# An MLP run per half of the tokens, with its up-projection as seven block products instead of eight

## The chip, the cores and the metric

One core of one Trainium2 chip runs the whole program. The metric is the device time of one execution in microseconds; the kernel before has a median of 2911.13 us over 3 runs (2910.79 to 2911.31).

## What is computed

Two layers of a small hybrid network over 1152 tokens (128 context tokens, then 1024 latent tokens) of width 1024. Each layer is a token mixer (attention, linear attention and a recurrent branch) and then an MLP with a hidden width of 4096 and squared ReLU:

```python
    h = rmsnorm(x, P['norm2'][l]) * (1.0 + sc2) + sh2
    u = jax.nn.relu(h @ P['w_mlp1'][l])          # 1024 -> 4096
    x = x + g2 * ((u * u) @ P['w_mlp2'][l])      # 4096 -> 1024
```

Scale, shift and gate differ between context and latent tokens. Only this part changes; the mixer, the final norm and the other outputs stay.

## The kernel before

Activations lie with the channels on the partitions: `x[k]` (k = 0 to 7) is 128 channels x 1152 tokens in SBUF. All large products are done in float32r (`F32R`) with a two-term split: each fp32 operand is cast to a high part (`wh`, `hh`, `uh`) and the rest is its low part (`wl`, `hl`, `ul`). One product of two 128-wide blocks is then three matmuls, high by high, high by low and low by high: lines 156, 157 and 158 of `dense`. `load_w` brings 1024 columns of weights by one DMA on SP's queue (`wr`), ACT casts them (L119), DVE takes the rest (L120).

The tokens are worked in three thirds of 384 (`TB`); `parts` cuts the first third at token 128, where scale and shift change. In `mlp`:

- `norm2(tb)` makes the modulated activations of one third, channel block by channel block (`norm`, L350 to L358), as a generator whose steps are put in between matmuls by `tick`. It needs the reciprocal root mean square of that third: `squares` (L300 to L306), the transposes L313 in `rstd`, the power L318 on POOL, and `spread` (L331 to L338), which spreads it over the partitions.
- `up_prep(f)` loads one 128-column tile f of the up-weights (32 tiles), `up_unit(f, tb)` multiplies it with one third (8 channel blocks x 3 matmuls of 384 columns) and makes ReLU and squares: ACT L1259 and L1260, POOL L1261, DVE L1262.
- `down_chunk(c, tbs)` multiplies four finished tiles with the down-weights (L1283 adds the gated result to x on DVE). Up and down are interleaved, four tiles at a time. `last_tb` starts the next layer's first norm for a third when its last chunk is done.

A weight tile is loaded and split once per layer and used for all three thirds. The first up tiles of a layer run third by third, so that the norm of the second and third thirds is made while the matmuls of the first run. `post_out` drives the end of the mixer's output projection (`out_half`, L1218 to L1225) and adds the norms as their thirds become ready.

PE's order is the order in which the code emits the matmuls. The order on DVE, ACT and POOL is made by a scheduler from the dependences and is fixed at build time; each of these engines runs its list in that order.

Of the kernel before, what the change touches and what calls it, by code (L numbers as in the profile page):

```python
# [7 lines left out]
F32 = mybir.dt.float32  # L8
F32R = mybir.dt.float32r
AF = mybir.ActivationFunctionType  # L10
ALU = mybir.AluOpType
# [3 lines left out]
D = 1024  # L15
KD = 8
TP = 128
# [2 lines left out]
NT = T // 128  # L20
TB = 384
NTB = T // TB
DEPTH = 2
DFF = 4096
EPS = 1e-6
# [22 lines left out]


class Net:  # L50
# [1177 lines left out]
    def mlp(self, l, post_out, last_tb, side_work=None):  # L1228
        nc, I = self.nc, self.I
        hg, hp = self.open(f"h2_{l}", bufs=1)  # L1230
        hh = [hp.tile([128, T], F32R, tag=f"hh{k}", name=f"hh{k}") for k in range(KD)]
        hl = [hp.tile([128, T], F32R, tag=f"hl{k}", name=f"hl{k}") for k in range(KD)]
        M = self.M[l]
        N2 = {}

        def norm2(tb):
            N2[tb] = self.add(self.norm(self.xa, tb, self.rs2, lambda: M["G2"], lambda: M["sh2"], lambda kt, b: blk(hh[kt], b),
                                        lambda kt, b: blk(hl[kt], b)))

        post_out(norm2)  # L1240
        ug, up = self.open(f"u_{l}", side="right", bufs=5)
        NF = DFF // 128
        CH = 4
        U = {}
        self.wide = True
        W = {}

        def up_prep(f):
            W[f] = self.load_w(I["w_mlp1"][l, :, f * 128:f * 128 + 128].rearrange("(k p) c -> p k c", p=128), KD)
            U[f] = (up.tile([128, T], F32R, tag="uh", name="uh"), up.tile([128, T], F32R, tag="ul", name="ul"))  # L1250

        def up_unit(f, tb):
            wh, wl = W[f]
            uh, ul = U[f]
            p = self.pd()
            self.dense(p[:, :TB], [wh[:, k] for k in range(KD)], [wl[:, k] for k in range(KD)],
                       [(blk(hh[k], tb), blk(hl[k], tb)) for k in range(KD)], True)
            r = self.te()
            nc.scalar.activation(r, p[:, :TB], AF.Relu)  # L1259
            nc.scalar.activation(blk(uh, tb), r, AF.Square)  # L1260
            nc.gpsimd.tensor_tensor(r, r, r, ALU.mult)  # L1261
            nc.vector.tensor_tensor(blk(ul, tb), r, f32(blk(uh, tb)), ALU.subtract)  # L1262

        def up_tile(f):
            up_prep(f)
            for tb in range(NTB):
                up_unit(f, tb)

        def down_chunk(c, tbs):
            fs = range(c * CH, c * CH + CH)  # L1270
            for dp in range(KD // 2):
                wh, wl = self.load_w(I["w_mlp2"][l, c * CH * 128:(c + 1) * CH * 128, dp * 256:dp * 256 + 256]
                                     .rearrange("(k p) c -> p k c", p=128), CH)
                for dd in range(2):
                    dt = 2 * dp + dd
                    for tb in tbs:
                        p = self.pd()
                        sl = slice(128 * dd, 128 * dd + 128)
                        self.dense(p[:, :TB], [wh[:, k, sl] for k in range(CH)], [wl[:, k, sl] for k in range(CH)],
                                   [(blk(U[f][0], tb), blk(U[f][1], tb)) for f in fs], True)  # L1280
                        for a, b, s in parts(tb):
                            xa = self.xa(dt, tb)[:, a:b]
                            nc.vector.scalar_tensor_tensor(xa, p[:, a:b], self.M[l]["g2"][:, dt, s:s + 1], xa, ALU.mult, ALU.add)  # L1283

        for f in range(2):
            up_prep(f)
        for tb in range(NTB):
            self.finish(N2[tb])
            for f in range(2):
                up_unit(f, tb)  # L1290
        if side_work:
            self.add(side_work())
        for f in range(2, CH + 1):
            up_tile(f)
        nch = NF // CH
        for c in range(nch):
            if c == nch - 1:
                self.drain()
                self.close(hg)
                for tb in range(NTB):  # L1300
                    down_chunk(c, [tb])
                    last_tb(tb)
            else:
                down_chunk(c, range(NTB))
            for f in range((c + 1) * CH + 1, min((c + 2) * CH + 1, NF)):
                up_tile(f)
        self.close(ug)

    def final_open(self):
# [74 lines left out]
    def layer(self, l, depth):  # L1384
        self.mixer(l)
        side = self.mod_round(l, 2, self.pe, slow=3)
        seq = [(0, 1), (1, 1), (2, 1), (0, 0), (1, 0), (2, 0)]
        done, state = set(), {"gen": None, "left": 0, "cur": None}
        nc = self.nc
        self.rs2 = {}  # L1390
        rs0 = self.norm_rs(self.xa, 0, self.rs2)

        def load_next(force):
            if seq and seq[0] not in self.ms and (force or seq[0][1] or seq[0][0] in done):
                assert seq[0][1] or seq[0][0] in done
# [36 lines left out]
        def post_out(norm2):  # L1432
            done.add(2)
            load_next(False)
            for _ in rs0:
                pass
            added = 0
            k = 0
            while out_step():
                k += 1  # L1440
                if added == 0:
                    norm2(0)
                    added = 1
                if added == 1 and (1, 0) not in seq and state["cur"] == (2, 0):
                    self.chain.insert(0, self.norm_rs(self.xa, 1, self.rs2, eng0=nc.vector))
                    norm2(1)
                    added = 2
                if k % 2 == 0:
                    self.tick()
            self.chain.insert(0, self.norm_rs(self.xa, 2, self.rs2, eng0=nc.vector))  # L1450
            norm2(2)
# [89 lines left out]
```

## Time and profile before

| | |
|---|---|
| median of 3 runs | 2911.13 us |
| profiled execution, its own time | 2908.05 us |
| its span in the profile | 2906.2 us |
| mean granted TensorE clock | 0.977 |
| PE busy | 2748.9 us (95%), 16067 matmuls |
| DVE, ACT, POOL busy | 1455.2 us (50%), 1119.6 us (39%), 802.5 us (28%) |

In a row, `x2006` is a count of instructions; shapes are partitions x elements. Matmuls are pipelined: a row's duration of one matmul is longer than the distance to the next one, so what a stream of matmuls costs is read from starts, or from a count in a stretch without idle time.

### The profile page before, as it was taken

The numbers are of one execution on the slowest core, as the hardware profiler recorded it, in microseconds if no ns is written. First come the engines' busy times: TensorE is split into PE (matmuls) and PEld (weight loads), VectorE is DVE, ScalarE is ACT, GpSimd is POOL, SyncE is SP. The second block draws the span as 40 slices with busy tenths as digits, with TensorE's granted clock in tenths as the row PEclk, the third lists the DMA queues.
The fourth block names the chain that finished last, engine by engine and source line by source line (L and its number), as shares of the span: only waits on it lengthen the run. The fifth ranks groups of instructions, "written<-read, shape, count | busy, mean of one in ns | idle before, by whom it ended". The sixth has DMA issues, their size and how long they took to land. (4 is left out here: it accounts for less than half of the span.)

```text
span 2906.2 us, 41527 instructions
## 1 busy us (share of the span) xinstructions
PE 2748.9 (95%) x16067; PEld 2625.6 (90%) x16067; DVE 1455.2 (50%) x2577; ACT 1119.6 (39%) x2046; POOL 802.5 (28%) x848
## 2 busy tenths in 40 slices
PE   5898899999999999999988989899899999999998
PEld 4887897889999999999987879878899999999998
DVE  7645677795332333233475547778832333233235
ACT  4645447763112212211356436477612112211223
POOL 4234447742001001100223244576311001100112
PEclk7999999999999999999999999999999999999999
DMA  7545358421321111111343643662211111111113
GB/s 263 137 124 158 99 157 253 128 80 51 95 88 38 43 44 44 44 37 44 111 120 86 175 127 102 217 210 69 73 37 44 44 44 39 42 44 44 44 37 131
DMA packets 279301, 273.64 MB, mean 94 GB/s; under 512 B 30032, under 2 KB 259008, under 8 KB 279104
## 3 DMA queue, kind: packets, MB, share of 16 engines
q1 hardware_dynamic: 278888, 270.92, 30.5%
q8 instruction: 127, 2.08, 0.3%
q14 instruction: 70, 0.57, 0.1%
q10 hardware_dynamic: 216, 0.06, 0.0%
HBM read 227.02 MB, written 43.91 MB: 93 GB/s over the span
## 5 line engine op out<-in xcount | busy, mean ns | idle before, releaser
L119 ACT CAST wh<-wr 128x1024 fp32r<-128x1024 f32 x228 | 239.0, 1048 | 923.5 <-PE pg L157 822.4
L157 PE MATMUL pg<-hl,wh 128*128 128x384 f32 x1584 | 538.3, 340 | 3.2 <-DVE hl L358 1.7
L156 PE MATMUL pg<-hh,wh 128*128 128x384 f32 x1584 | 538.4, 340 | 1.8 <-ACT hh L351 1.8
L158 PE MATMUL pg<-hh,wl 128*128 128x384 f32 x1584 | 537.3, 339 | 0.0
L1261 POOL TENSOR_TENSOR te<-te 128x384 f32<-128x384 f32 x192 | 165.9, 864 | 1332.9 <-ACT uh L1260 1332.7
L158 PE MATMUL pg<-uh,wl 128*128 128x384 f32 x1536 | 513.5, 334 | 1.7 <-DVE wl L120 1.7
L156 PE MATMUL pg<-uh,wh 128*128 128x384 f32 x1536 | 514.4, 335 | 0.6 <-ACT wh L119 0.6
L157 PE MATMUL pg<-ul,wh 128*128 128x384 f32 x1536 | 513.2, 334 | 0.0
L1283 DVE SCALAR_TENSOR_TENSOR x<-pg,mod,x 128x384 f32<-128x384 f32 (+2 forms) x512 | 254.2, 515 | 395.7 <-PE pg L158 395.4
L120 DVE TENSOR_TENSOR wl<-wr,wh 128x1024 fp32r<-128x1024 f32 x196 | 245.1, 1251 | 213.0 <-ACT wh L119 213.0
L1262 DVE TENSOR_TENSOR ul<-te,uh 128x384 fp32r<-128x384 f32 x192 | 107.1, 558 | 453.4 <-POOL te L1261 453.4
L156 PE MATMUL pd<-hh,wh 128*128 128x384 f32 x816 | 295.3, 362 | 22.2 <-DVE te L491 11.1
L157 PEld LDWEIGHTS pg<-hl,wh 128*128 128x128 f32 x1584 | 299.1, 189 | 5.6 <-DVE hl L358 3.0
L156 PEld LDWEIGHTS pg<-hh,wh 128*128 128x128 f32 x1584 | 299.3, 189 | 5.4 <-issue 3.4
L158 PEld LDWEIGHTS pg<-hh,wl 128*128 128x128 f32 x1584 | 299.3, 189 | 0.0
L156 PEld LDWEIGHTS pg<-uh,wh 128*128 128x128 f32 x1536 | 288.3, 188 | 4.3 <-DVE x L1283 1.7
L158 PEld LDWEIGHTS pg<-uh,wl 128*128 128x128 f32 x1536 | 288.3, 188 | 2.3 <-DVE wl L120 2.2
L157 PEld LDWEIGHTS pg<-ul,wh 128*128 128x128 f32 x1536 | 288.4, 188 | 0.0
L157 PE MATMUL pd<-hl,wh 128*128 128x384 f32 x816 | 285.1, 349 | 3.4 <-DVE hl L392 3.4
L158 PE MATMUL pd<-hh,wl 128*128 128x384 f32 x816 | 284.0, 348 | 0.0
L1259 ACT ACTIVATE te<-pg 128x384 f32<-128x384 f32 x192 | 93.8, 489 | 360.2 <-PE pg L158 360.2
L156 PEld LDWEIGHTS pd<-hh,wh 128*128 128x128 f32 x816 | 161.3, 198 | 30.7 <-DVE te L491 12.1
(279 smaller groups left out, 4341.7 us busy)
## 6 DMA issues: line engine op xcount, KB each, us to landing
wr<-in_w_mlp_dram SPq DMA_DIRECT2D x144, 512.0 KB, 4.0
wm<-in_w_mod_dram SPq DMA_DIRECT2D x96, 512.0 KB, 4.9
wr<-in_w_out_dram SPq DMA_DIRECT2D x48, 512.0 KB, 4.9
wr<-in_w_in_dram SPq DMA_DIRECT2D x36, 512.0 KB, 5.2
xd<-x SPq DMA_DIRECT2D x48, 192.0 KB, 3.6
x<-xd SPq DMA_DIRECT2D x48, 192.0 KB, 3.9
raw<-mixd SPq DMA_DIRECT2D x40, 192.0 KB, 2.9
B<-gkd SPq DMA_DIRECT2D x16, 288.0 KB, 4.6
```

The costliest lines, as they stand in the source:

```text
L119: nc.scalar.copy(hi[:, :m], raw[:, :m])
L120: lo_eng.tensor_tensor(lo[:, :m], raw[:, :m], f32(hi[:, :m]), ALU.subtract)
L156: mm(out, wh[i], xs[i][0], start=i == 0, stop=False)
L157: mm(out, wh[i], xs[i][1], start=False, stop=False)
L158: mm(out, wl[i], xs[i][0], start=False, stop=i == n - 1)
L1259: nc.scalar.activation(r, p[:, :TB], AF.Relu)
L1261: nc.gpsimd.tensor_tensor(r, r, r, ALU.mult)
L1262: nc.vector.tensor_tensor(blk(ul, tb), r, f32(blk(uh, tb)), ALU.subtract)
L1283: nc.vector.scalar_tensor_tensor(xa, p[:, a:b], self.M[l]["g2"][:, dt, s:s + 1], xa, ALU.mult, ALU.add)
```

## The change

The up-projection is cut into 2 x 2 blocks three ways: the 8 channel blocks into two halves of 4, a pair of weight tiles (2p, 2p+1), and a half of the tokens (576) into two quarters of 288 (`TW`). Eight block products become seven (a form of Strassen's scheme) over sums of weight blocks and of activation blocks. The MLP runs first for one half of the tokens, then for the other, and both weight matrices are loaded, summed and split once per half.

- `norm2(half)` multiplies x with the spread root (POOL for channel blocks 0 to 3, DVE for 4 to 7), scales on ACT, forms the sums (L1254 to L1257, alternating POOL and DVE) and splits seven operands of 288 columns into `HH` and `HL` (L1260). It goes in four steps kk, each working in `R[0]` (a buffer of tag `wr`) and `R[1]` (tag `er`, of which there is one).
- `up_prep(p)` loads the pair's two tiles, forms three sums of 512 columns on POOL (L1313 to L1316, four instructions), and splits 3 x 1024 + 512 columns (ACT cast, DVE L1295). Raw tiles rotate through `wr`, `wr`, `er`.
- `up_pair(p)` runs the seven products (each 4 x 3 matmuls of 288 columns) in the order 1, 2, 6, 5, 3, 7, 4 and combines them on DVE (L1346, L1359), then ReLU and square on ACT, L1349 on POOL, L1350 on DVE.
- `down(half, fs, tts)` does the down-projection of 4 (twice per half 2) tiles for one half, in four pieces of weights.

Core of the diff:

```diff
+TW = 288
...
-        hh = [hp.tile([128, T], F32R, tag=f"hh{k}", name=f"hh{k}") for k in range(KD)]
-        hl = [hp.tile([128, T], F32R, tag=f"hl{k}", name=f"hl{k}") for k in range(KD)]
+        HH = [hp.tile([128, 7 * TW], F32R, name=f"ch{k}") for k in range(4)]
+        HL = [hp.tile([128, 7 * TW], F32R, name=f"cl{k}") for k in range(4)]
...
+        def norm2(half):
+            h0 = 2 * TW * half
+            pbs = []
+            for tb in range(half, half + 2):
+                pbs.append(((yield from self.spread(self.rs2[tb], self.tn)), tb))
+            for kk in range(4):
+                R = (self.wp.tile([128, 1024], F32, tag="wr", name="ra"), hp.tile([128, 4 * TW], F32, tag="er", name="er"))
+                for j in range(2):
+                    k = kk + 4 * j
+                    eng = nc.vector if j else nc.gpsimd
+                    for pb, tb in pbs:
+                        lo, hi = max(h0 - tb * TB, 0), min(h0 + 2 * TW - tb * TB, TB)
+                        c = tb * TB - h0
+                        eng.tensor_tensor(R[j][:, c + lo:c + hi], self.xa(k, tb)[:, lo:hi], pb[:, lo:hi], ALU.mult)
+                    for a, b, s in ((0, TP, 0), (TP, 2 * TW, 1)) if half == 0 else ((0, 2 * TW, 1),):
+                        d = R[j][:, a:b]
+                        nc.scalar.activation(d, d, AF.Identity, bias=M["sh2"][:, k, s:s + 1], scale=M["G2"][:, k, s:s + 1])
+                u = lambda j, i: R[j][:, TW * i:TW * i + TW]
+                nc.gpsimd.tensor_tensor(u(0, 2), u(1, 1), u(0, 1), ALU.subtract)
+                nc.vector.tensor_tensor(u(0, 1), u(0, 1), u(0, 0), ALU.subtract)
+                nc.vector.tensor_tensor(u(1, 2), u(1, 1), u(0, 1), ALU.subtract)
+                nc.gpsimd.tensor_tensor(u(1, 3), u(1, 0), u(1, 2), ALU.subtract)
+                for r, c, n in ((R[0], 0, 3 * TW), (R[1], 3 * TW, 4 * TW)):
+                    nc.scalar.copy(HH[kk][:, c:c + n], r[:, :n])
+                    nc.vector.tensor_tensor(HL[kk][:, c:c + n], r[:, :n], f32(HH[kk])[:, c:c + n], ALU.subtract)
+                yield
...
+        def split(r, m=1024, hl=None):
+            h, lo = hl or (rot(1, HT, F32R), rot(2, LT, F32R))
+            h, lo = h[:, :m], lo[:, :m]
+            nc.scalar.copy(h, r[:, :m])
+            nc.vector.tensor_tensor(lo, r[:, :m], f32(h), ALU.subtract)
+            return h, lo
...
+            tt = nc.gpsimd.tensor_tensor
+            w = split(r1)
+            W[p] = Wp = {1: half(w, A), 2: half(w, B)}
+            tt(s1, r2[:, A], r2[:, B], ALU.add)
+            tt(r2[:, A], r1[:, A], r2[:, A], ALU.subtract)
+            tt(r1[:, A], s1, r1[:, A], ALU.subtract)
+            tt(r1[:, B], r1[:, B], r1[:, A], ALU.subtract)
+            w = split(r1)
+            Wp[6], Wp[3] = half(w, A), half(w, B)
+            Wp[5] = split(s1, 512, (ep.tile([128, 512], F32R, tag="h1", name="h1"), ep.tile([128, 512], F32R, tag="l1", name="l1")))
+            w = split(r2)
+            Wp[7], Wp[4] = half(w, A), half(w, B)
...
+            for k in range(4):
+                c = slice(128 * k, 128 * k + 128)
+                mm(out, wh[:, c], HH[k][:, xs], start=k == 0, stop=False)
+                mm(out, wh[:, c], HL[k][:, xs], start=False, stop=False)
+                mm(out, wl[:, c], HH[k][:, xs], start=False, stop=k == 3)
+            self.tick()
...
+        for half in range(2):
+            up_prep(0)
+            for g in self.h2s:
+                self.finish(g)
...
+            for p in range(NPR):
+                up_pair(p)
+                if p == NPR - 2:
+                    down(half, range(2 * p - 4, 2 * p - 2))
+                elif p % 2 == 0 and p:
+                    down(half, range(2 * p - 4, 2 * p))
+                if p + 1 < NPR:
+                    up_prep(p + 1)
+            if half == 0:
+                self.h2s = [self.add(norm2(1))]
+            else:
                 self.drain()
...
+                last_tb(0)
+            down(half, range(NF - 6, NF - 4))
+            if half == 0:
+                down(half, range(NF - 4, NF))
             else:
+                for tt in range(2):
+                    down(half, range(NF - 4, NF), (tt,))
+                    last_tb(1 + tt)
```

How the order moves, at three places. First DVE in layer 0, where the mixer's output projection ends (its additions to x are L1225 before, L1226 in the change). Before, the rows between them belong to the norm of single thirds, on separate buffers `tn`:

```order
L120 TENSOR_TENSOR wl<-wr,wh 128x1024
L350 SCALAR_TENSOR_TENSOR tn<-x_3702,G_5516,tn 128x384
L1225 SCALAR_TENSOR_TENSOR x_3708<-pd,mod_1_2797,x_3708 128x384
L350 SCALAR_TENSOR_TENSOR tn<-x_3704,G_5516,tn 128x384
L352 SCALAR_TENSOR_TENSOR hl_6217<-tn,mod_1_2797,hh_6209 128x384
L358 TENSOR_TENSOR hl_6218<-tn,hh_6210 128x384
```

In the change each step kk runs from L1249 to its second L1260, and the next step's L1249 writes the one `er` that this L1260 has read:

```order
L1226 SCALAR_TENSOR_TENSOR x_3707<-pd,mod_1_2797,x_3707 128x384
L1249 TENSOR_TENSOR er<-x_3707,tn 128x384
L1249 TENSOR_TENSOR er<-x_3707,tn 128x192
L305 TENSOR_TENSOR tn<-tn 128x384 x3
L1255 TENSOR_TENSOR ra<-ra 128x288
L305 TENSOR_TENSOR tn<-tn 128x384
L1256 TENSOR_TENSOR er<-er,ra 128x288
L1260 TENSOR_TENSOR cl_6214<-ra,ch_6210 128x864
L1260 TENSOR_TENSOR cl_6214<-er,ch_6210 128x1152
L1249 TENSOR_TENSOR er<-x_3708,tn 128x384
```

So the four steps follow one another on DVE, with the output projection's and the third third's work (L305) in between. Second POOL, at the first pair of the first half. Before, POOL had the product of the norm and the product of an up tile here, and no work for the weights:

```order
L354 TENSOR_TENSOR tn<-x_3705,tn 128x384
L354 TENSOR_TENSOR tn<-x_3707,tn 128x384
L1261 TENSOR_TENSOR te<-te 128x384
L318 TENSOR_TENSOR rs<-ms,nhalf 128x3
L1261 TENSOR_TENSOR te<-te 128x384
```

In the change it is this (`s_6628` is the first pair's `s1`):

```order
L1249 TENSOR_TENSOR ra<-x_3705,tn 128x192
L1254 TENSOR_TENSOR ra<-er,ra 128x288
L1257 TENSOR_TENSOR er<-er 128x288
L1313 TENSOR_TENSOR s_6628<-wr 128x512
L1349 TENSOR_TENSOR te<-te 128x288
L1314 TENSOR_TENSOR wr<-wr 128x512
L1315 TENSOR_TENSOR wr<-s_6628,wr 128x512
L1316 TENSOR_TENSOR wr<-wr 128x512
```

L1349 belongs to the first pair's product 2, and the sums L1314 to L1316, from which the weights of products 6, 3, 7 and 4 are split, stand behind it. Third DVE where the first half ends and the second begins, in layer 0. Before, there was no such place; in the middle of the MLP the splits of weights stood between finished up and down tiles:

```order
L1283 SCALAR_TENSOR_TENSOR x_3709<-pg,mod_2_5513,x_3709 128x384 x2
L120 TENSOR_TENSOR wl<-wr,wh 128x1024
L1262 TENSOR_TENSOR ul<-te,uh 128x384 x2
L120 TENSOR_TENSOR wl<-wr,wh 128x1024
L1262 TENSOR_TENSOR ul<-te,uh 128x384 x3
L120 TENSOR_TENSOR wl<-wr,wh 128x1024
```

In the change the splits of 512 columns are pieces 2, 4 and 3 of the down-weights of `down(0, 26..27)`, and the steps kk = 1 to 3 of `norm2(1)` lie around them (rows between the two stretches are left out by the fences):

```order
L1249 TENSOR_TENSOR er<-x_3707,tn 128x384
L1255 TENSOR_TENSOR ra<-ra 128x288
L1295 TENSOR_TENSOR el<-wr,eh 128x512
L1256 TENSOR_TENSOR er<-er,ra 128x288
L1260 TENSOR_TENSOR cl_6214<-ra,ch_6210 128x864
```

```order
L1249 TENSOR_TENSOR er<-x_3709,tn 128x384
L1255 TENSOR_TENSOR ra<-ra 128x288
L1295 TENSOR_TENSOR el<-wr,eh 128x512
L1256 TENSOR_TENSOR er<-er,ra 128x288
L1260 TENSOR_TENSOR cl_6216<-ra,ch_6212 128x864
L1260 TENSOR_TENSOR cl_6216<-er,ch_6212 128x1152
L1295 TENSOR_TENSOR wl<-er,wh 128x512
L1295 TENSOR_TENSOR wl<-wr,wh 128x1024
```

So piece 2's split stands in step 1, and piece 3's, whose raw tile is the `er` that the norm uses, behind step 3.

## Rows read from the trace of the kernel before

**Rows 1.** The page, parts 1 and 4: busy time by engine, chain that ended last.

```profile
span 2906.2 us, 41527 instructions
PE 2748.9 (95%) x16067; PEld 2625.6 (90%) x16067; DVE 1455.2 (50%) x2577; ACT 1119.6 (39%) x2046; POOL 802.5 (28%) x848
PE 35%; DVE 3%; ACT 2%; issue 2%; POOL 2%; DMA 1%; SPq 0%; POOLq 0%; DVEq 0%; ACTq 0%
```

**Rows 2.** Windows over the two MLPs: stretch, us, then busy us of each engine.

```profile
core 0: us, PE busy (x) PEld busy (x) DVE busy (x) ACT busy (x) POOL busy (x), PEclk, DMA share, GB/s
656.00:1473.00 817.00, 812.64 (x4653) 801.59 (x4652) 300.99 (x513) 191.44 (x316) 100.58 (x112) 1.00 0.20 61
2070.00:2893.00 823.00, 818.06 (x4706) 815.93 (x4705) 294.63 (x475) 195.38 (x319) 107.48 (x121) 1.00 0.16 49
```

**Rows 3.** Window inside the first MLP, matmuls of 384 columns alone.

```profile
1050.00:1400.00 350.00, 350.00 (x2006) 350.00 (x2005) 112.67 (x183) 68.81 (x108) 34.28 (x40) 1.00 0.14 43
```

**Rows 4.** Timeline of PE at 565 us: 512-column matmuls, first and eighth start.

```profile
565.29 0.39 PE L1080 MATMUL pg<-kh,qs 128*128 128x512 f32 x1
...
566.91 0.39 PE L1080 MATMUL pg<-kl,qs 128*128 128x512 f32 x1
```

**Rows 5.** Timeline of PE at 434 us: 128-column matmuls, first and fourth start.

```profile
434.50 0.27 PE L1080 MATMUL pg<-kh,qs 128*128 128x128 f32 x1
...
434.83 0.27 PE L1080 MATMUL pg<-kl,qs 128*128 128x128 f32 x1
```

**Rows 6.** Groups by line and form: DVE, ACT, POOL (busy us, mean ns).

```profile
L120 DVE TENSOR_TENSOR wl<-wr,wh 128x1024 fp32r<-128x1024 f32 x196 | 245.1, 1251 | 213.0 <-ACT wh L119 213.0
L1262 DVE TENSOR_TENSOR ul<-te,uh 128x384 fp32r<-128x384 f32 x192 | 107.1, 558 | 453.4 <-POOL te L1261 453.4
L119 ACT CAST wh<-wr 128x1024 fp32r<-128x1024 f32 x228 | 239.0, 1048 | 923.5 <-PE pg L157 822.4 <-PE pd L157 69.1 <-PE pd L1219 20.1
L356 ACT ACTIVATE tn<-tn,mod,G 128x384 f32<-128x384 f32 x21 | 14.8, 703 | 13.0 <-POOL tn L354 13.0
L1261 POOL TENSOR_TENSOR te<-te 128x384 f32<-128x384 f32 x192 | 165.9, 864 | 1332.9 <-ACT uh L1260 1332.7
L120 POOL TENSOR_TENSOR wl<-wr,wh 128x1024 fp32r<-128x1024 f32 x32 | 76.9, 2404 | 36.2 <-ACT wh L119 36.0
```

**Rows 7.** Timelines of PE, DVE and POOL at the start of layer 1's MLP.

```profile
2057.22 0.52 PE L313 MATMUL pe<-ident,tn 128*128 128x128 f32 x3 [1.69 <-DVE tn L306]
2057.77 0.56 DVE L315 TENSOR_REDUCE ms<-pe 128x3 f32<-128x384 f32 x1 [0.17 <-PE pe L313]
2058.75 1.02 POOL L318 TENSOR_TENSOR rs<-ms,nhalf 128x3 f32<-128x3 f32 x1 [3.69 <-DVE ms L316]
2065.40 1.63 POOL L354 TENSOR_TENSOR tn<-x,tn 128x384 f32<-128x384 f32 x1 [5.63 <-ACT tn L338]
2066.08 1.37 DVE L350 SCALAR_TENSOR_TENSOR tn<-x,G,tn 128x384 f32<-128x384 f32 x1
2067.90 0.60 DVE L350 SCALAR_TENSOR_TENSOR tn<-x,G,tn 128x384 f32<-128x384 f32 x1
2076.33 1.35 DVE L306 TENSOR_TENSOR tn<-tn 128x384 f32<-128x384 f32 x1
2077.83 0.52 PE L313 MATMUL pe<-ident,tn 128*128 128x128 f32 x3 [3.01 <-DVE tn L306]
```

**Rows 8.** Windows behind that wait: columns as in the windows above.

```profile
2078.40:2081.80 3.40, 3.40 (x12) 3.40 (x11) 3.40 (x8) 0.29 (x1) 1.09 (x1) 0.50 0.01 2
2081.80:2085.20 3.40, 3.40 (x22) 3.37 (x22) 1.86 (x5) 2.51 (x5) 0.96 (x2) 1.00 0.00 0
```

**Rows 9.** Waits of PE, 1405 to 1480 us, the end of layer 0's MLP.

```profile
PE pg L158 <- DVE wl L120: 1.7, 1, 1.7
PE pe L313 <- DVE tn L306: 1.0, 1, 1.0
PE pg L156 <- ACT wh L119: 0.6, 1, 0.6
```

**Rows 10.** The page, part 6: DMA issues, the MLP's weight tiles.

```profile
wr<-in_w_mlp_dram SPq DMA_DIRECT2D x144, 512.0 KB, 4.0
```

More of the change, by code (lines that the diff above doesn't have):

```diff
@@ L1242, in mlp @@
+        post_out(lambda: self.add(norm2(0)))
+        ug, up = self.open(f"u_{l}", side="right", bufs=6)
+        eg, ep = self.open(f"e_{l}", bufs=1)
         NF = DFF // 128
[L1243 removed]
         U = {}
         self.wide = True
[L1246 to L1250 removed]
@@ L1252, in up_unit @@
[L1252 to L1262, printed above, removed]
@@ L1285, in mlp, with rot @@
[L1285 to L1297, printed above, removed]
+        nr = [0] * 4
+        RT, HT, LT = ["wr", "wr", "er"], ["wh", "eh"], ["wl", "el"]
+        more = [True]
+        def rot(i, tags, dt):
+            tag = tags[nr[i] % len(tags)] if more[0] else tags[0]
+            nr[i] += 1
+            if tag == "er":
+                return hp.tile([128, 4 * TW], F32, tag="er", name="er")[:, :1024]
+            if tag[0] == "e":
+                return ep.tile([128, 1024], dt, tag=tag, name=tag, bufs=2)
+            return self.wp.tile([128, 1024], dt, tag=tag, name=tag)
@@ new lines, in bank, with raw @@
+        def bank():
+            nr[3] += 1
+            if nr[3] % 7 < 5:
+                return self.pg()
+            return self.psp.tile([128, 512], F32, tag="pd", name="pd", bufs=2)
+        def raw():
+            return rot(0, RT, F32)
+        def split(r, m=1024, hl=None):
[4 more added lines that the diff above has]
+            return h, lo
@@ new lines, in mlp, with up_prep @@
+        W = {}
+        def up_prep(p):
+            R = []
+            for f in (2 * p, 2 * p + 1):
+                r = raw()
+                nc.sync.dma_start(r.rearrange("p (k c) -> p k c", k=KD), I["w_mlp1"][l, :, f * 128:f * 128 + 128].rearrange("(k p) c -> p k c", p=128))
+                R.append(r)
+            r1, r2 = R
+            s1 = ep.tile([128, 512], F32, tag="s1", name="s1")
+            A, B = slice(0, 512), slice(512, 1024)
+            tt = nc.gpsimd.tensor_tensor
+            half = lambda w, c: tuple(v[:, c] for v in w)
+            w = split(r1)
[9 more added lines that the diff above has]
+            Wp[7], Wp[4] = half(w, A), half(w, B)
@@ new lines, in mlp, with prod @@
+        XC = {1: 0, 2: 3, 3: 4, 4: 6, 5: 1, 6: 5, 7: 2}
+        def prod(p, j, out):
+            mm = nc.tensor.matmul
+            wh, wl = W[p][j]
+            xs = slice(TW * XC[j], TW * XC[j] + TW)
+            for k in range(4):
[4 more added lines that the diff above has]
+            self.tick()
@@ new lines, in up_pair, with act, one, plus @@
+        def up_pair(p):
+            us = []
+            for f in (2 * p, 2 * p + 1):
+                U[f] = (up.tile([128, 2 * TW], F32R, tag="uh", name="uh"), up.tile([128, 2 * TW], F32R, tag="ul", name="ul"))
+                us.append(U[f])
+            tw = lambda t: t[:, :TW]
+            def act(e, t, x, y):
+                uh, ul = (v[:, TW * t:TW * t + TW] for v in us[e])
+                r = tw(self.te())
+                nc.vector.tensor_tensor(r, x, y, ALU.add)
+                nc.scalar.activation(r, r, AF.Relu)
+                nc.scalar.activation(uh, r, AF.Square)
+                nc.gpsimd.tensor_tensor(r, r, r, ALU.mult)
+                nc.vector.tensor_tensor(ul, r, f32(uh), ALU.subtract)
+            def one(j):
+                o = tw(bank())
+                prod(p, j, o)
+                return o
+            def plus(o, x):
+                y = tw(self.tn())
+                nc.vector.tensor_tensor(y, o, x, ALU.add)
+                return y
+            s = tw(self.tn())
+            nc.scalar.copy(s, one(1))
+            act(0, 0, one(2), s)
+            u2 = plus(one(6), s)
+            v = plus(one(5), u2)
+            act(0, 1, one(3), v)
+            o = one(7)
+            w = plus(o, u2)
+            act(1, 1, o, v)
+            act(1, 0, one(4), w)
@@ new lines, in mlp @@
+        NPR = NF // 2
+        for half in range(2):
+            up_prep(0)
+            for g in self.h2s:
+                self.finish(g)
+            if half == 0 and side_work:
+                self.add(side_work())
+            for p in range(NPR):
[9 more added lines that the diff above has]
+            else:
@@ L1436, in post_out @@
                 pass
-            added = 0
             k = 0
+            self.h2s = []
             while out_step():
                 k += 1
[L1441 to L1444, printed above, removed]
+                if not self.h2s and (1, 0) not in seq and state["cur"] == (2, 0):
                     self.chain.insert(0, self.norm_rs(self.xa, 1, self.rs2, eng0=nc.vector))
[L1446 to L1451, printed above, removed]
+                    self.h2s.append(norm2())
+                self.tick()
+            self.add(self.norm_rs(self.xa, 2, self.rs2, eng0=nc.vector))
             self.close(self.kg)
```

52 lines of the change are left out of this document (22 added, 30 removed).

## The prediction

> **What bounds the kernel now.** I read the page's busy times and chain first [rows 1]: TensorE is busy for 95% of the span, and of the chain that ended last PE is the only large part (35%). So the MLP's price is a count of matmuls times a spacing, if nothing starves PE. The windows over the two MLPs say that nothing does [rows 2]: 812.64 of 817 us and 818.06 of 823 us busy, at a granted clock of 1.00, while DVE, ACT and POOL are busy for about 300, 193 and 104 us. The window inside the first MLP [rows 3] gives the spacing: 350.00 us for 2006 matmuls of 384 columns, 174.5 ns each. The other rows price what the change puts beside PE.
>
> **The matmul stream.** Before, a layer has 32 up tiles x 3 thirds x 24 matmuls and as many for down, 4608 of 384 columns: 4608 x 174.5 ns = 804.1 us. After, up is 2 halves x 16 pairs x 7 products x 12 = 2688, and down is 2 halves x 2 quarters x 8 output blocks x 32 tiles x 3 = 3072: 5760 of 288 columns. In columns that is 6% less (up by 1/8, down unchanged), with 1152 more instructions. No matmul of 288 columns is in the trace. Eight starts of 512 columns lie 231 ns apart [rows 4], so from 384 to 512 columns one column costs (231 - 174.5) / 128 = 0.44 ns; carried down by 96 columns this gives 132, and in proportion to the 174.5 it is 131. At 128 columns the spacing is 110 ns [rows 5], twice what columns alone would cost, so some floor per matmul acts there; a straight line from that row to 384 gives 150, the upper bound. I take 133, since 288 columns are nearer to 384 and well above the floor. The lower bound is 120, 288 columns at 2.4 GHz with no gap. Then 5760 x 133 = 766.1 us: **-38.0 a layer, -76 in all**. One ns of spacing is 11.5 us over both layers.
>
> **The start of a layer's first half.** Each product needs all four channel groups, so nothing can start before all of `norm2(0)` is done, where before the first third's norm was enough. A step kk is a chain through the single `er`: DVE's two multiplications (384 columns 0.56, 192 about 0.30), ACT's scaling of 576 columns (0.70 for 384, so about 0.9), POOL's first sum (288 columns, three quarters of 0.86, about 0.7), two DVE sums of 0.43, POOL's second (0.7), the ACT cast of 1152 columns (1.05 x 1.125 = 1.2) and DVE's rest of them (1.25 x 1.125 = 1.4) [rows 6]: 6.6, and six changes of engine at 0.1 (DVE's L306 ends at 2077.68, L313 starts 0.15 later [rows 7]), so 7.2 to 7.3. Four steps are 29 us, and nothing of one step can overlap the next on `er`. The chain starts when the second third's root is spread. That root is made 2.6 us after L313's start (L318 ends at 2059.77 [rows 7]); a copy, three transposes and a copy, about 0.5 each as L315 and L313 are, bring it to 5 us. In DVE's list the output projection's last additions and the third third's squares lie in between, some 5 us more: the norm is ready about 39 us after L313. PE has then only 78 matmuls of the projection left, 13.6 us: 25 us idle. Products 1 and 2 then take 3.2 us, and product 6 waits for the summed weights, because POOL's L1349 (after product 2's DVE add, ReLU and square) stands ahead of L1314 to L1316: 1.3 for the first two, 0.7 for L1349, 3 x 1.2 for the sums (half of POOL's 2.40 [rows 6]), 1.05 and 1.25 for cast and split, 7.5 us after hops. The wait of 3.0 us for the third third's root that stands here today [rows 7] goes, since it now lies in this gap. After such a wait the clock is low: behind that one PE ran a stretch of 3.4 us at a granted 0.50, the 1.2 GHz level, with 12 matmuls where the next 3.4 us held 22 [rows 8], a loss of 1.7; here two such restarts, 3.4. 25 + 7.5 - 3.0 + 3.4 = **+33 a layer**. Without the insertions and with the weights' wait at half it is 25.
>
> POOL's multiplications of the next step run beside DVE's of this one. The trace shows what that can do: L350 took 1.37 us where POOL's L354 ran beside it, and 0.60 alone [rows 7]. I have not put this into 29; if each step lost two such 0.8 us, a chain would be 6 longer, 24 over the four chains. The Trainium skill, SBUF — State Buffer, "Who interferes with whom", says why: a VectorE instruction with two SBUF inputs and a GpSimd one that reads SBUF exclude each other for the whole instruction. By that rule these four chains come out at the long end.
>
> **The switch of halves.** `norm2(1)` is issued when the first half's products are over. Beside it PE has `down` of tiles 26 and 27, four pieces of 24 matmuls (3.2 us each), then of 28 to 31. But DVE's list has the split of piece 2 in step 1 of the norm, of piece 4 in step 3, and of piece 3 behind step 3, because its raw tile is the `er` itself: its DMA can start only after the last step. A tile of twice its size took 4.0 us to land [rows 10]; I say 3. So piece 3 starts at 3.5 (first additions, ahead of step 0) + 29 + 3 + 0.6 + 0.65 and some hops and additions, about 40 us, and PE has 6.5 us of work till then: 33.5 idle, and 1.7 of clock: **+35 a layer**. The lower end is 27, if the steps run at their bare 7.2 and the DMA lands in 2; the upper one 42, with the blocking above. Hiding this would need work that is ready: the pieces of tiles 28 to 31 stand behind it in PE's order.
>
> **The end of a layer.** At the end of layer 0 PE waits 1.7 + 1.0 + 0.6 today [rows 9]. In the change a piece's split stands behind the next layer's first norm in DVE's list, which I put at 15 us of idle time; **+12**, between 0 and 15. At the end of layer 1 I put nothing: the final norm's work is as before.
>
> **The steady state** I cost at nothing. Two pairs and a `down` of four tiles are 360 matmuls, 48 us at 133 ns. DVE has in them 10 splits of 1024 columns at 1.25 (6 for up, 4 for down) and 2 of 512 at 0.65, 22 combinations and 16 gated additions of about 0.45: 31 us in all. ACT has 10 casts of 1.05, 2 of 0.55 and 18 instructions of about 0.42, 19; POOL 8 sums of 1.2 and 8 products of 0.65, 15 (all by columns from [rows 6]). Even if every POOL instruction kept DVE waiting, 31 + 15 = 46 is under 48. The weights come in 512 KB tiles, 8 in 48 us, with 4.0 us for one [rows 10]. If this cover fails, each cycle loses what DVE lacks.
>
> **The sum** is against the profiled execution, 2908.05 us, which is 3 us (0.1%) below the median: 2908 - 76 + 2 x (33 + 35) + 12 = 2980, or 2983 on the scale of the median.
>
> **Rivals.** (1) *The floor of the short matmuls acts at 288 columns too*: 150 ns. The 110 ns at 128 columns speaks for a floor, but 384 and 512 columns lie almost in proportion, which speaks against it. 5760 x 150 = 864 a layer, +120 in all instead of -76: 3179. (2) *DVE and POOL become the bound*: against it stand 31 us of 48, for it that DVE's splits wait for ACT's casts in a fixed list and POOL's rows stand between them. With 2 us lost in each of 28 of the 32 cycles, +56: 3039. (3) *It gets faster, by the spacing*: with the gap per matmul of 384 columns (174.5 - 160 = 14.5 ns) gone at 288, it is 120 ns, 5760 x 120 = 691 a layer, -226 in all, and with the same stalls 2833. It decides at 126.7 ns, where the stream gives 148 us, what the stalls cost. Rows 3 and 4 speak against it: the gap did not vanish at either width. The Trainium skill, TensorE: Matmul & The Clock Gate, "Back-to-back issue gap", gives N / 2.4 + 2.5 ns for an isolated matmul, an estimate of 122.5 at 288 columns (2862 in all); for 384 it gives 162.5, where the trace has 174.5, so here it does not hold. That the change doesn't do what it says I leave out: the counts above are those of the order listing. That the stalls cancel the stream's gain to within 0.2% (about 6 us, what a measurement of this kernel can tell from no change) needs 72 us less of them, half of their sum; it has a small chance.
>
> **How the numbers follow.** Forecast 0.72, rival 1 0.05, rival 2 0.09, rival 3 0.10, no change 0.04. The forecast has 23 us either way for 2 ns of spacing, and from the stalls' ends -44 (8 at each of the four chains, 12 at the layer's end) to +29 (6 or 7 at each chain, 3 at the end); not all at once, so about 2925 to 3030. The range takes in rival 2 and leaves out rivals 1 and 3: 2920 to 3050. Faster 0.11, same 0.04, slower 0.85.
>
> **What would show it.** In the changed profile: matmuls of 288 columns 131 to 135 ns apart at clock 1.00; at the start of each MLP a gap of some 25 us that DVE's L1260 ends, then one of 7 that ends at the weights' split L1295; at the switch, waits for L1295 of 33 us together; DVE under 70% busy between. It is wrong if the spacing is over 140 or under 128, if the steps kk overlap, or if waits of PE for L1295 run through the whole MLP.

## The result, and the profile after

The change is slower: 3005.24 us (median of 4 runs, 3000.58 to 3010.73) against 2911.22 us (2910.79 to 2912.44), a ratio of 1.0323, 95% interval 1.0305 to 1.0341. Forecast were 2983 us and a range of 2920 to 3050. The profiled execution took 3005.05 us; its span is 96.8 us longer than that of the kernel before.

Page of the change, parts 1 and 4 [rows 1]:

```profile
span 3003.0 us, 49043 instructions
PE 2703.1 (90%) x18377; PEld 2573.2 (86%) x18377; DVE 2032.4 (68%) x3567; ACT 1407.0 (47%) x2500; POOL 1213.8 (40%) x1212
PE 12%; issue 1%; POOL 1%; ACT 1%; DVE 1%; DMA 0%; POOLq 0%; ACTq 0%; DVEq 0%
```

PE is busy for 46 us less and the span is 97 us longer: PE now waits more. Two windows inside the up- and down-projections, as in [rows 3]:

```profile
1100.00:1400.00 300.00, 300.00 (x2264) 300.00 (x2263) 205.98 (x325) 118.29 (x194) 111.40 (x106) 1.00 0.32 97
2200.00:2480.00 280.00, 280.00 (x2113) 280.00 (x2112) 193.84 (x345) 108.36 (x178) 100.52 (x96) 1.00 0.29 86
```

280.00 / 2113 is 132.5 ns a matmul of 288 columns, and PE does not wait once in either window; DVE is 69% busy. The stream gained about what was forecast, and the steady state is covered. The loss is at the edges. Waits of PE at the start of layer 0's MLP (629 to 712 us), the four longest:

```profile
PE pd L1219 <- ACT wh L120: 16.1, 1, 16.1
PE pg L1331 <- ACT eh L1294: 8.2, 1, 8.2
PE pg L1331 <- DVE s4b L222: 2.9, 1, 2.9
PE pg L1333 <- DVE wl L1295: 2.4, 1, 2.4
```

At the switch of halves in layer 0 (1040 to 1100 us):

```profile
PE pg L157 <- ACT wh L1294: 21.3, 1, 21.3
PE pd L157 <- ACT eh L1294: 11.3, 1, 11.3
PE pe L337 <- DVE tn L332: 2.1, 1, 2.1
PE pd L159 <- DVE el L1295: 0.7, 1, 0.7
```

And at the end of layer 0 (1460 to 1552 us), where [rows 9] had 3.3 us in all:

```profile
PE pg L159 <- DVE wl L1295: 7.0, 2, 6.8
PE pe L314 <- DVE tn L307: 5.7, 1, 5.7
PE pg L159 <- DVE wl L121: 3.4, 1, 3.4
```

To compare kernels I use the **time above the stream**: over a stretch between fixed places of the program, the distances between successive matmul starts, less 174.5, 133, 231 and 110 ns for each of 384, 288, 512 and 128 columns. "Start" is the last block of the output projection and the first 300 up matmuls; "switch" the 450 matmuls ahead of the second half and its first 300; "end" the last 520 matmuls and, in layer 0, the next mixer's first part.

| us above the stream, layer 0 / 1 | start | switch | end |
|---|---|---|---|
| before | 9 / 9 | - | 27 / 3 |
| the change | 42 / 43 | 41 / 40 | 46 / 12 |
| no_second_norm | 41 / 42 | 1 / 2 | 46 / 12 |
| norm_own_buffer | 36 / 35 | 39 / 39 | 46 / 12 |
| pieces_ahead | 41 / 43 | 26 / 25 | 47 / 11 |
| both_buffer_and_ahead | 36 / 36 | 25 / 24 | 46 / 12 |
| norm_steps_apart | 30 / 31 | 31 / 30 | 47 / 12 |
| steps_apart_and_ahead | 29 / 30 | 25 / 23 | 48 / 12 |
| first_pair_by_blocks | 36 / 42 | 32 / 32 | 46 / 11 |
| paced_and_early_root | 30 / 30 | 19 / 18 | 36 / 14 |
| projection_last | 22 / 23 | 19 / 19 | 34 / 14 |
| projection_last_paced | 18 / 18 | 22 / 20 | 39 / 15 |
| six_tiles_a_group | 21 / 22 | 26 / 24 | 35 / 14 |
| norm_sums_on_dve | 18 / 19 | 21 / 19 | 37 / 13 |

For the change the differences to before are 33 + 34, 41 + 40 and 19 + 9, together 176; less the 76 of the stream, at the 133 ns that the table takes for 288 columns, that is 100, against the 97 measured. (The expectations below quote some of these from narrower stretches.)

### The profile page after: what moved, and what is told of

It reads as the page before. It is cut to its first block, busy times and chain, and to the rows that moved or that the text cites. A ratio compares the mean times of both kernels' runs of the same rounds, so it can differ in the third digit from the quotient of the medians.

```text
span 3003.0 us, 49043 instructions
## 1 busy us (share of the span) xinstructions
PE 2703.1 (90%) x18377; PEld 2573.2 (86%) x18377; DVE 2032.4 (68%) x3567; ACT 1407.0 (47%) x2500; POOL 1213.8 (40%) x1212
## 5 line engine op out<-in xcount | busy, mean ns | idle before, releaser
L1349 POOL TENSOR_TENSOR te<-te 128x288 f32<-128x288 f32 x256 | 182.1, 719 | 498.0 <-ACT uh L1348 489.7
L157 PE MATMUL pd<-hh,wh 128*128 128x384 f32 x816 | 296.0, 363 | 24.0 <-DVE te L492 10.7
L1393 DVE SCALAR_TENSOR_TENSOR x<-pg,mod,x 128x128 f32<-128x128 f32 (+1 forms) x516 | 217.1, 449 | 117.6 <-PE pg L159 117.2
L157 PE MATMUL pg<-uh,wh 128*128 128x288 f32 x788 | 237.2, 301 | 42.7 <-ACT wh L1294 42.7
L1350 DVE TENSOR_TENSOR ul<-te,uh 128x288 fp32r<-128x288 f32 x256 | 176.0, 703 | 134.9 <-POOL te L1349 132.8
L1294 ACT CAST wh<-wr 128x1024 fp32r<-128x1024 f32 (+1 forms) x134 | 133.6, 997 | 278.8 <-PE pg L158 151.3
L159 PE MATMUL pg<-uh,wl 128*128 128x288 f32 x788 | 236.1, 300 | 7.0 <-DVE wl L1295 7.0
L158 PE MATMUL pg<-ul,wh 128*128 128x288 f32 x788 | 235.5, 299 | 0.0
L157 PE MATMUL pg<-uh,eh 128*128 128x288 f32 x680 | 200.9, 295 | 1.5 <-DVE x L1393 1.5
L159 PE MATMUL pg<-uh,el 128*128 128x288 f32 x680 | 201.1, 296 | 0.0
L158 PE MATMUL pg<-ul,eh 128*128 128x288 f32 x680 | 200.7, 295 | 0.0
L1294 ACT CAST eh<-wr 128x1024 fp32r<-128x1024 f32 (+1 forms) x106 | 107.4, 1013 | 184.4 <-PE pg L158 79.0
L157 PEld LDWEIGHTS pd<-hh,wh 128*128 128x128 f32 x816 | 161.8, 198 | 32.6 <-DVE te L492 11.3
L1295 DVE TENSOR_TENSOR wl<-wr,wh 128x1024 fp32r<-128x1024 f32 (+1 forms) x134 | 158.4, 1182 | 42.7 <-ACT wh L1294 42.4
L1331 PE MATMUL pg<-ch,eh 128*128 128x288 f32 x544 | 163.2, 300 | 22.0 <-ACT eh L1294 16.1
```

What stands on the lines that cost most here:

```text
L157: mm(out, wh[i], xs[i][0], start=i == 0, stop=False)
L158: mm(out, wh[i], xs[i][1], start=False, stop=False)
L159: mm(out, wl[i], xs[i][0], start=False, stop=i == n - 1)
L1294: nc.scalar.copy(h, r[:, :m])
L1295: nc.vector.tensor_tensor(lo, r[:, :m], f32(h), ALU.subtract)
L1331: mm(out, wh[:, c], HH[k][:, xs], start=k == 0, stop=False)
```

## The experiments

All are edits of the change. Single runs stood beside a run of the kernel before of 2906.7 to 2912.5 us. The four runs of the change span 10 us, so a few us between two single runs show nothing by themselves; there the waits and the table decide.

**no_second_norm** leaves out the norm of the second half, so that half multiplies the first half's activations.

```diff
-                self.h2s = [self.add(norm2(1))]
+                self.h2s = []
```

> Leaves out the norm of the second half of the tokens (the second half multiplies the first half's normalised activations). Theory (the wait at the switch of halves is the norm's chain, with the splits of the down pieces queued behind it): the waits of PE at the two switches, 40 and 39 us above the stream, fall under 6 each, and the time to about 2932 us (3005 - 73). Rival (the pieces' weights are late of themselves, because both weight matrices are now loaded and split twice): PE still waits for the casts and splits L1294 and L1295 for over 20 us at each switch, and the time stays above 2965.

Measured: 2918.5 us. At both switches PE's waits are gone. All that is left of them at the first, 1000 to 1110 us:

```profile
PE pg L157 <- DVE x L1393: 0.6, 1, 0.6
```

So the doubled loads and splits do not by themselves make PE wait; the norm does, and it costs 87 us over both layers, more than the stream gains.

**norm_own_buffer** takes the norm's R[0] out of the two raw weight tiles.

```diff
-R = (self.wp.tile([128, 1024], F32, tag="wr", name="ra"), ...
+R = (hp.tile([128, 3 * TW], F32, tag="ra", name="ra"), ...
-s1 = ep.tile([128, 512], F32, tag="s1", name="s1")
+s1 = hp.tile([128, 3 * TW], F32, tag="ra", name="s1")[:, :512]
```

> The norm's R[0] gets a buffer of its own in place of one of the two raw weight tiles (the sum s1 shares it; nothing is left out). Theory (the 16 us wait of the output projection and part of the 8 us wait of product 6 come from raw tiles that the norm holds): the wait of L1219 falls from 16 to under 3, the wait of product 6 from 8 to under 5, but the first product still waits for the four steps, so that only 5 to 12 us a layer are won: 2981 to 2995. Rival (POOL's order, L1349 ahead of the sums, makes the product 6 wait): that wait stays at 7 to 8 us and the time within 2996 to 3008.

Measured: 2988.0 us. The waits at the start of layer 0:

```profile
PE pg L1331 <- ACT ch L1259: 13.2, 2, 6.8
PE pg L1331 <- ACT eh L1294: 4.9, 1, 4.9
PE pd L1219 <- DVE x L1226: 4.4, 1, 4.4
PE pg L1332 <- DVE cl L1260: 2.8, 3, 1.3
```

The 16.1 us of the output projection were the raw tile that the norm held; they are now 4.4, for another reason. In their place the first product waits for the norm's casts (L1259) and splits (L1260) step by step. The chain sets most of the start, as forecast: it fell by only 6 and 8 us, and for the rest the buffer had moved the place where PE waits. Product 6's wait (L1294's cast into `eh`) fell to 4.9, with L1349 still ahead of L1314 on POOL.

**pieces_ahead** loads and splits the eight pieces at the switch up to three ahead, in `wr` alone.

```diff
+                while len(ws) < min(i + 1 + la, len(todo)):
+                    ws.append(piece(todo[len(ws)][0], todo[len(ws)][2]))
...
+                RT[:] = ["wr"]
+                down(half, (range(NF - 6, NF - 4), both), (range(NF - 4, NF), both), la=3)
```

> At the switch of halves the eight pieces of down-weights are loaded and split up to three pieces ahead, in the raw tiles that the norm's R[1] does not use. Theory (the order on DVE and the shared buffer make the wait; PE has 38 us of down-projection that can cover the norm): the time above the stream at the switch falls from 40 to 5 to 15 us, the time to 2945 to 2965. Rival (the norm's chain is then later by the splits put ahead of it, and the first product of the second half waits in place of the pieces): 25 to 35 us stay at the switch, now as a wait of the first products for L1259 or L1260, and the time stays above 2980.

Measured: 2976.2 us, between the two. The long waits for pieces went, but 26 and 25 us stayed, 9.0 of the first still for a cast of weights, as the norm then works in `wr` too; with a buffer for the norm, in the next run, that wait is gone.

**both_buffer_and_ahead** joins the two, and issues the norm's steps at the switch four ticks apart.

> Both edits, and the norm's steps at the switch issued four ticks apart. Theory: the gains add, 2925 to 2950. Rival (both edits only move the wait to the norm's chain): above 2970.

Measured: 2960.1 us, 10 over the upper end. The gains add (17 and 29 us alone, 45 together), but the switch is still 25 above the stream. Its longest wait is now for DVE's gated additions, which free PSUM banks:

```profile
PE pg L157 <- DVE x L1401: 5.7, 3, 2.8
PE pe L337 <- DVE tn L332: 2.5, 1, 2.5
```

**norm_steps_apart** gives steps 1 and 2 memory of their own (that of the fourth step's result).

```diff
+                if kk in (1, 2):
+                    q = hp.tile([128, 7 * TW], F32, tag="cl3" if kk == 1 else "ch3", name="rq")
+                    R = (q[:, :3 * TW], q[:, 3 * TW:])
```

> As norm_own_buffer, and steps 1 and 2 of the norm work in memory that only the fourth step's result needs later, so that successive steps no longer wait for the one buffer er (nothing is left out, the down pieces stay behind the norm as in the change). Theory (the chain is serial because of er): the four steps take 18 to 24 us in place of 35 to 38; the time above the stream falls by 8 to 14 us at each of the four places, 2988 to 2935-2955. Rival (the steps are bound by DVE, ACT and POOL and by POOL's blocking of DVE, not by the buffer): under 4 us at each place, 2972 to 2988.

Measured: 2963.1 us against 2988.0, 8 over the upper end of the theory and below the rival's 2972: 4 to 9 us at each place. On DVE the change has the four steps start at 633.67, 645.18, 653.95 and 662.56 and end at 671.27, 37.6 us:

```profile
633.67 0.89 DVE L1249 TENSOR_TENSOR er<-x,tn 128x384 f32<-128x384 f32 x1
...
645.18 0.81 DVE L1249 TENSOR_TENSOR er<-x,tn 128x384 f32<-128x384 f32 x2
...
653.95 0.83 DVE L1249 TENSOR_TENSOR er<-x,tn 128x384 f32<-128x384 f32 x2
...
662.56 1.10 DVE L1249 TENSOR_TENSOR er<-x,tn 128x384 f32<-128x384 f32 x2
...
669.93 1.34 DVE L1260 TENSOR_TENSOR cl<-er,ch 128x1152 fp32r<-128x1152 f32 x1
```

Here they take from 634.26 to 662.56, 28.3 us:

```profile
634.26 0.89 DVE L1253 TENSOR_TENSOR er<-x,tn 128x384 f32<-128x384 f32 x1
...
643.57 1.99 DVE L1267 TENSOR_TENSOR cl<-er,ch 128x1152 fp32r<-128x1152 f32 x1 [0.30 <-ACT ch L1266]
...
661.22 1.34 DVE L1267 TENSOR_TENSOR cl<-er,ch 128x1152 fp32r<-128x1152 f32 x1
```

The one buffer `er` cost 9 of 37 us. The rest is the engines' own work and their blocking, which this run does not tell apart. That there is blocking the rows show: the same split of 1152 columns takes 1.99 us at 643.57, where a POOL instruction had begun ahead of it, and 1.34 at 661.22, where it began first; there POOL's sum of 512 columns, begun after it, took 2.34, and the next such sum 1.26. POOL's rows of the same stretch:

```profile
643.35 0.99 POOL L1253 TENSOR_TENSOR ra<-x,tn 128x384 f32<-128x384 f32 x1 [1.00 <-DVE cl L1267]
...
661.37 2.34 POOL L1320 TENSOR_TENSOR s<-wr 128x512 f32<-128x512 f32 x1 [2.13 <-DVE cl L1267]
663.79 1.26 POOL L1321 TENSOR_TENSOR wr<-wr 128x512 f32<-128x512 f32 x1
```

**steps_apart_and_ahead** joins this with pieces_ahead, also at the end (one piece ahead).

> norm_steps_apart and pieces_ahead together, with the pieces at the end of the layer one ahead too. Theory: the switch, at 15 us above the stream in both_buffer_and_ahead, falls under 8; the start to 20 to 26; the end of layer 0, 29 above the stream, to 15 to 25 because its pieces' splits no longer stand behind the next norm: 2905 to 2935. Rival (the end's wait is the next norm itself): the end stays at 27 to 33, the time 2925 to 2950.

Measured: 2947.5 us, 12 over. The end did not move (46 to 48), nor did the switch beyond pieces_ahead's: with all steps issued at once, PE's waits there are now for the additions on DVE (14.8 of 17.3 us in layer 0).

**first_pair_by_blocks** runs the first pair's seven products channel block by channel block.

> As steps_apart_and_ahead, and the first pair of each half runs channel block by channel block over its seven products (21 matmuls a step in place of 3) so that PE has work while the later steps are made. Theory (the first product waits for each step, then six more products stand behind the last): of the 11 us of the first pair 5 to 8 lie beside the norm, 10 to 25 us less than steps_apart_and_ahead over both layers. Rival (the sums of the first pair's weights come last, not the norm): PE waits for L1302's splits there, and the time is within 6 us of steps_apart_and_ahead.

Measured: 2979.3 us, 32 slower, a miss: the first matmuls now need all seven sets of weights. At the start of layer 0 the wait for L1301's cast of summed weights rose from 6.5 us to 8.9, and PE's wait for the third third's root (L314) from 3.8 to 7.6. The second half's start, where the same pair comes, rose from 25 and 23 above the stream to 32.

**paced_and_early_root** issues the steps at the switch three ticks apart, keeps four split buffers for the last pieces, and makes the first third's root for the next layer in the second half.

> As steps_apart_and_ahead, with the norm's steps at the switch issued three ticks apart, four split buffers kept for the last down pieces, and the root of the first third for the next layer made during the second half. Theory: the switch falls from 23 us above the stream to 8 to 15, the end of layer 0 from 36 to 20 to 27: 2947 to 2910-2925. Rival (DVE and POOL have too little room for norm and splits together at these places, in whatever order): the switch stays above 20 and the end above 32, 2938 to 2950.

Measured: 2930.9 us, 6 over. The end fell from 48 to 36, the switch from 25 and 23 to 19 and 18. The rival is part of the truth: what is left at the switch is again DVE's additions (9.9 of the 12.4 us of waits).

**projection_last** moves one block of the output projection behind the second third's.

```diff
-        seq = [(0, 1), (1, 1), (2, 1), (0, 0), (1, 0), (2, 0)]
+        seq = [(0, 1), (1, 1), (0, 0), (1, 0), (2, 1), (2, 0)]
```

> As paced_and_early_root, and the output projection's block of the third third's first half of channels moves behind the second third's, so that PE has 96 more matmuls (16.7 us) while the first norm is made. Theory (the start's wait is lack of ready matmuls beside the norm): the start falls from 29 us above the stream by 10 to 16 in each layer, 20 to 32 us less than paced_and_early_root. Rival (the attention stage needs that block as filler): the stall appears there, above 5 us a layer in the stretch ahead of the MLP, and less than 10 us is won in all.

Measured: 2938.0 us, 7 slower. The start fell to 22 and 23, but the stretch of the attention and the blocks ahead of it rose from 14 and 15 above the stream to 27 and 23: the rival. Of the 22 that are left at the start, 10.7 are one wait, for the cast of the projection's weights, which ACT's list had behind the norm's casts.

**projection_last_paced** issues the first norm's steps five ticks apart.

> As projection_last, with the steps of the first norm issued five ticks apart so that the projection's weights are cast ahead of the later steps, and the early root and the spread at the switch given more ticks before PE needs them. Theory (in projection_last the 11 us wait was ACT's list: the cast of the projection's weights behind the norm's casts): the start falls from 28 and 24 us above the stream to 8 to 16 in each layer, the early root's 4.5 us to under 1.5: 2938 to 2898-2918. Rival (the waits only move to the first products, because norm, casts and splits fill DVE): the start stays above 20 in each layer, 2922 to 2938.

Measured: 2926.7 us (4 runs), ratio to before 1.0056, interval 1.0039 to 1.0073. The start fell to 18 and the early root's wait went, but the third third's root is now waited for in the first pairs, 4.1 us, and the attention's stretch stayed at 23. The time is the rival's. DVE is nearly full there: 44.04 us busy of the 50 around the first norm, 48.28 of the 60 around the switch.

```profile
1030.00:1090.00 60.00, 47.07 (x313) 45.47 (x312) 48.28 (x86) 25.33 (x30) 26.34 (x24) 0.89 0.32 97
620.00:670.00 50.00, 36.95 (x199) 33.77 (x197) 44.04 (x53) 31.09 (x45) 28.78 (x23) 0.94 0.28 83
```

**six_tiles_a_group** puts a half's last six tiles into one accumulation group, with the steps at the switch four ticks apart and the third third's root made later.

> As projection_last_paced (steps four ticks apart at the switch), and the last six up tiles of a half go through the down-projection in one accumulation group in place of two, which halves the gated additions there, and the third third's root is made some pairs later. Theory (at the switch DVE, with norm, splits and additions, has more work than PE's 38 us): the switch falls from 20 us above the stream to 8 to 14, the end of layer 0 from 27 to 16 to 23, and the 4.5 us wait for the third root goes: 2927 to 2888-2908, at or below the kernel before. Rival (the additions are not what DVE lacks; the norm's chain through ACT and POOL is): the switch stays at 17 to 20, 2912 to 2922.

Measured: 2940.7 us (5 runs), ratio 1.0111, interval 1.0095 to 1.0126: slower by 14, a miss. Without the group of the two older tiles PE needs the last pair's squares at once (waits of 2.1 us for L1356 and 1.5 for L1358 at the switch), and the second half's first weights come later (3.6 and 1.7 for L1302). Which of the three edits did it was not tried apart.

**norm_sums_on_dve** moves the norm's two POOL sums to DVE.

> As projection_last_paced, with the two of the four sums of each norm step that POOL made (L1254 and L1257 in the change) on DVE: 16 instructions of 0.8 us a layer off POOL, 16 of 0.43 onto DVE. Theory (DVE and POOL keep each other waiting in the norm, and each step crosses to POOL and back twice): the steps are 1 to 2 us shorter, the start and the switch together 4 to 10 us a layer less above the stream, 2927 to 2907-2919. Rival (DVE is what is full at these places): no gain or a loss of up to 4 us a layer, 2924 to 2936.

Measured: 2925.7 us (5 runs), ratio 1.0051, interval 1.0038 to 1.0065: no difference to projection_last_paced, as the rival said. The switch fell by about 1 us in each layer, the start did not. DVE is busy for 52.85 us in the same 60 around the switch, where it had been 48.28. That fits work that comes out even with the blocking taken away; the two were not separated.

No version beats the kernel before; the best two are 0.5 to 0.6% slower.

## Why the prediction was right, and where its sizes were off

- **The stream.** 133 ns were forecast and 132.5 measured, which makes 82 us where 76 were forecast. The two rivals that rested on this number (150 and 120 ns) are out. Nor does the formula of the Trainium skill for an isolated matmul (TensorE: Matmul & The Clock Gate, "Back-to-back issue gap"), 122.5 ns at 288 columns, give the spacing of this stream.
- **The steady state** was costed at nothing: no wait of PE in 300 us, DVE at 69% where 31 of 48 us (65%) had been worked out. Rival 2 is out.
- **The start**, +33 a layer, came to 33 and 34. Counted from the second third's root (L314), products 1 and 2 were over after 44 us, where 39 + 3.2 + 1.7 had been worked out, and product 6 then waited 8.2 us, where 7.5 were forecast (the terms listed for it add up to 7.9 before any hop):

```profile
629.50 0.52 PE L314 MATMUL pe<-ident,tn 128*128 128x128 f32 x3 [1.00 <-DVE tn L307]
...
673.28 0.29 PE L1333 MATMUL pg<-ch,wl 128*128 128x288 f32 x1
681.73 0.61 PE L1331 MATMUL pg<-ch,eh 128*128 128x288 f32 x1 [8.16 <-ACT eh L1294]
```

  Inside this sum two errors cancelled, which was luck: the norm ended 42 us after L314 and not 39, but product 1 did not wait for all of it, as the text had said, and ran beside the fourth step from 666.21 on. The place of the wait was wrong too. The text had PE run the projection's 78 matmuls and then wait for the norm. It waited inside the projection, 16.1 us, because step and projection share the raw tiles, a dependence that I had not followed. norm_own_buffer shows that the chain sets most of the total. The 8.2 us for product 6 were forecast through POOL's L1349. But L1313, ahead of it, waited for the raw tile, and the wait fell to 4.9 with the norm's buffer; the order on POOL was at most part of it.
- **The switch**, +35, came to 41 and 40. Pieces 2 and 3 waited as forecast, in two waits of 11.3 and 21.3 us. The term that was mis-sized is the step: 7.2 to 7.3 us, 29 for four. In the change the steps at the switch begin at 1047.14, 1057.80, 1068.07 and 1075.38 and end at 1083.86, so one took 7.3 and the others 8.5 to 10.7, 36.7 in all. Piece 3 began 45.5 us after the first half's products, where about 40 had been worked out:

```profile
1041.93 0.29 PE L157 MATMUL pg<-uh,wh 128*128 128x288 f32 x1
...
1087.44 0.61 PE L157 MATMUL pg<-uh,wh 128*128 128x288 f32 x1 [21.32 <-ACT wh L1294]
```

  POOL's rows of the change, with one of DVE, show what the longer steps hold:

```profile
1048.05 2.32 POOL L1249 TENSOR_TENSOR ra<-x,tn 128x384 f32<-128x384 f32 x2 [1.27 <-ACT tn L339]
...
1053.48 1.06 DVE L1260 TENSOR_TENSOR cl<-ra,ch 128x864 fp32r<-128x864 f32 x1
1053.50 1.69 POOL L1257 TENSOR_TENSOR er<-er 128x288 f32<-128x288 f32 x1 [1.49 <-DVE er L1256]
...
1061.75 2.47 POOL L1249 TENSOR_TENSOR ra<-x,tn 128x192 f32<-128x192 f32 x2 [1.23 <-issue]
1064.18 0.80 POOL L1257 TENSOR_TENSOR er<-er 128x288 f32<-128x288 f32 x1
...
1071.98 0.79 POOL L1257 TENSOR_TENSOR er<-er 128x288 f32<-128x288 f32 x1 [1.20 <-DVE er L1256]
...
1079.71 1.57 POOL L1257 TENSOR_TENSOR er<-er 128x288 f32<-128x288 f32 x1 [1.61 <-DVE er L1256]
```

  The step's last sum, L1257, took 0.79 in the step of 7.3 us. In the first and the last step it took 1.69 and 1.57, because DVE's split of 864 columns had begun just ahead of it (at 1053.48 and 1079.58); in the second it stood behind POOL's multiplications for the next step, 2.47 us, and began 2.2 us late. These are about 4 of the 7.5 us by which the steps exceed four times 7.3. Some 2 more lie in the first step, where POOL's multiplications had to wait until the second third's root was spread (L339). So the blocking of [rows 7], named in the prediction and left out of the 29, belonged in it: with that place in POOL's list it makes about half of what was missing. This agrees with the Trainium skill's rule (SBUF — State Buffer, "Who interferes with whom"): in these rows the one that began first ran at its own time (DVE's split 1.06), and the other waited. Taking POOL's sums away (norm_sums_on_dve) won nothing all the same.
- **The clock.** At the switch the 1.7 us hold: the window behind the 21.3 us has 13 matmuls at a granted 0.50, the 1.2 GHz level, the next 24. Behind the 16.1 us at the start the low clock lasted longer:

```profile
656.70:665.17 8.47, 7.25 (x22) 6.74 (x22) 7.02 (x8) 4.72 (x8) 5.31 (x4) 0.50 0.23 64
...
1087.40:1090.80 3.40, 3.35 (x13) 3.13 (x14) 2.50 (x4) 0.94 (x1) 0.00 (x0) 0.50 0.40 126
1090.80:1094.20 3.40, 3.40 (x24) 3.40 (x24) 1.68 (x4) 0.97 (x2) 0.00 (x0) 0.85 0.60 187
```

  The 22 matmuls of 384 columns took 7.25 us, 3.4 more than at 174.5 ns, where a restart had been put at 1.7. As PE then waited for the first product's weights all the same (2.4 us, L1295), the difference can have cost little.

- **The ends**, +12 and 0, came to 19 and 9. Layer 0's pieces stood behind the next norm as forecast (7.0 us); not seen were the root of the first third, 5.7, which comes only when the second half is done, and the next mixer's weights, 3.4. paced_and_early_root took 10 of the 19 back. At the end of layer 1 I put nothing, "the final norm's work is as before"; but it too starts later against the matmuls: PE waits 3.0 us there for L307, where before it had no such wait. Where the rest of these 9 us comes from was not tried.
- **Was the loss to be had back?** Of the 176 us the edits of order and buffers took about 80. What stays is work that the kernel before did beside the stream and that the change needs in one go at four places: about 37 us of norm on DVE, ACT and POOL, while the splits and additions of the matmuls that should cover it need the same engines. Whether a form of the change that makes the second half's sums earlier would do better was not tried; it would need memory for a second set of operands.

## What to carry to other kernels

A scheme that saves matmuls at the price of sums over whole operands turns a rolling preparation into a barrier: count not only its instructions but the time from its last input to its last output, and what PE has ready meanwhile. Look for that price at every place where operands change hands, here four, and check for each buffer on that chain who else draws from it, since a shared raw tile or a fixed list puts the wait in front of other work. The steady state, in which the saving is real, says nothing of this: here it gained about 80 us, and the second norm alone cost 87.

## What the runs showed of the hardware that was not expected

The spacing of matmuls stays almost proportional below 384 columns: 132.5 ns at 288 (0.460 ns a column) beside 174.5 at 384 (0.454) and 231 at 512 (0.451), so the 110 ns at 128 columns are a floor that does not yet act at 288. Where between the two it begins no row here shows. And where an instruction of DVE with two inputs in SBUF and one of POOL that reads SBUF overlapped in the rows above, they did not slow each other a little: the one that began second was longer by about what the first still ran, POOL's sum of 288 columns 1.69 us in place of 0.79.
